# Prefix-flow step on one core: second layer's modulation vectors summed on DVE in the first MLP, norm transposes placed later

## Chip, core and metric

The kernel runs on one core of a Trainium2 chip. The metric is the device time of one execution in microseconds; the time of a kernel is the median of its runs.

## What is computed

One inference step of a flow-matching network of two layers. 1152 tokens (128 of context, 1024 latent) have 1024 channels each. A layer is a token mixer (windowed attention, gated linear attention, a gated recurrence) and an MLP with 4096 hidden channels, each behind a normalization that shift, scale and gate vectors modulate:

```python
def ada_mod(cond, w_mod, b_mod):
    mod = jax.nn.silu(cond) @ w_mod + b_mod
    mod = mod.reshape(-1, 1, 6 * D_MODEL)
    return jnp.split(mod, 6, axis=-1)

def layer(x, cond, l, P, ctx):
    sh1, sc1, g1, sh2, sc2, g2 = ada_mod(cond, P['w_mod'][l], P['b_mod'][l])
    h = rmsnorm(x, P['norm1'][l]) * (1.0 + sc1) + sh1
    mix, new_ctx = token_mixer(h, l, P, ctx)
    x = x + g1 * mix
    h = rmsnorm(x, P['norm2'][l]) * (1.0 + sc2) + sh2
    u = jax.nn.relu(h @ P['w_mlp1'][l])
    x = x + g2 * ((u * u) @ P['w_mlp2'][l])
    return x, new_ctx
```

There are two conditioning vectors, one for the context tokens and one for the latent ones. So the modulation of a layer is a product of two vectors with a 1024x6144 fp32 matrix: little arithmetic, 25 MB of weights.

## The kernel before

**Data.** x lies in SBUF as eight tiles of 128 channels by 1152 tokens. Tokens go in three blocks (tb 0 to 2) of 384. Every large product splits its fp32 operands into a high and a low part and takes three matmuls, high by high, low by high and high by low: lines L161 to L163 (`dense`), where the names hh, hl are the two parts of a normalized activation, uh, ul those of the hidden one and wh, wl those of a weight. The output projection has its own three, L1225 to L1227.

**Order.** PE's order is written by hand: it is the order in which the program emits matmuls. Small work that has to run beside the large products is written as generators that stand in `self.chain`; `tick` takes one step of the first one, and `dense` calls it every 12 matmuls. A bare `yield` is therefore "twelve matmuls later". The other engines' orders (DVE, ACT, POOL, and SP, which starts the loads) are made by a scheduler from modelled times, so an operation that is ready early can be listed far ahead of where the program emits it.

**Modulation vectors.** They are computed in three rounds of 2048 columns: round 0 gives the shift and gain of the first norm, round 1 the first gate and the second shift, round 2 the second gain and gate. `mod_round` (L246) loads, for each of eight 128-row pieces of the weight, two tiles of 128x1024 (`wm`, two buffers) and then issues four matmuls L261, one per 512 columns. In these the conditioning (`cs`, 128x32, of which two columns are filled) is the stationary operand, the weight streams, and each of the four writes 32 rows of one PSUM bank from its own 32 columns of the array:

```python
for g in range(4):
    nc.tensor.matmul(p[32 * g:32 * g + 32, :], self.cs[:, kt, :], ws[g // 2][:, 512 * (g % 2):512 * (g % 2) + 512],
                     start=kt == 0, stop=kt == KD - 1, tile_position=(0, 32 * g))
```

`mod_fin` (L265) copies the bank to SBUF (`mrow`; ACT L268, DVE L269), transposes it by four matmuls (L273) and adds the bias on DVE. For the second layer, round 0 runs in the first layer's MLP (`side_work`, one piece every eight steps), round 1 in the second layer's mixer (from the projection named gk1 to the one named k), round 2 in the second layer's attention (`side` in `layer`).

**Norms.** For one token block, `squares` (L297) squares the eight tiles on ACT and adds them on POOL and DVE (last addition L311). `norm_rs` lets two steps pass, and `rstd` (L314) then transposes the sum by three matmuls (L318) into the one PSUM bank `pe`, reduces it on DVE (L320, L321) and takes the power on POOL (L323). `spread` (L333) copies the result to 128 columns (DVE L336), lets one step pass, and transposes back (three matmuls L341; ACT copies to SBUF, L343). `norm` (L346) then makes hh and hl of each channel tile, half of them with DVE, ACT, DVE (L355 to L357), half with POOL, ACT, DVE (L359 to L363). These steps run at three borders: from attention and output projection to the MLP in both layers (`post_out`; the output projection's results are added to x by DVE, L1232), and from the first MLP to the second layer's mixer (`last_tb`).

**MLP.** `up_unit` is 24 matmuls and four operations on ACT, POOL and DVE (L1266 to L1269). `down_chunk` is 12 matmuls for each of eight output tiles and three blocks, added to x by DVE (L1290). Weights come by `load_w`: load L123 on SP, high part on ACT (L124), low part on DVE or POOL (L125), two buffers of each.

Of the kernel before, what the change touches and what calls it, by code (L numbers as in the profile page):

```python
# [15 lines left out]
KD = 8  # L16
# [33 lines left out]
class Net:  # L50
# [190 lines left out]
    def mod_round(self, l, r, psum, pool=None, slow=1):  # L241
# [20 lines left out]
                                 start=kt == 0, stop=kt == KD - 1, tile_position=(0, 32 * g))  # L262
        yield from self.mod_fin(l, r, p)

    def mod_fin(self, l, r, p):  # L265
        nc = self.nc
        m = self.wp.tile([128, 1024], F32, tag="wm", name="mrow")[:, :512]
        nc.scalar.copy(m[:, :256], p[:, :256])  # L268
        nc.vector.tensor_copy(m[:, 256:], p[:, 256:])  # L269
        yield  # L270
        p2 = self.pe()
        for j in range(4):
            nc.tensor.transpose(p2[:, 128 * j:128 * j + 128], m[:, 128 * j:128 * j + 128], self.ident)  # L273
        mt = self.const.tile([128, 4, 4, 2], F32, name=f"mod{l}_{r}")
        bm = self.V[l]["vt"][:, V_BMOD + 16 * r:V_BMOD + 16 * r + 16].rearrange("p (g j) -> p g j", g=4)
        src = p2.rearrange("p (j g s) -> p g j s", j=4, g=4)
        for s in range(2):
            nc.vector.tensor_tensor(mt[:, :, :, s], src[:, :, :, s], bm, ALU.add)
        M = self.M.setdefault(l, {})
        m = mt.rearrange("p g j s -> p (g j) s")  # L280
        if r == 0:
            M["sh1"] = m[:, 0:8]
            M["G1"] = self.gains(l, "G1", m[:, 8:16], V_N1)
        elif r == 1:
            M["g1"], M["sh2"] = m[:, 0:8], m[:, 8:16]
        else:
            M["G2"] = self.gains(l, "G2", m[:, 0:8], V_N2)
            M["g2"] = m[:, 8:16]
# [34 lines left out]
        nc.gpsimd.tensor_tensor(rs, ms, self.nhalf[:, :3], ALU.pow)  # L323
        return rs

    def norm_rs(self, x, tb, ret, alloc=None, eng0=None):
        acc = self.squares(x, tb, alloc, eng0)
        for _ in range(2):
            yield
        ret[tb] = self.rstd(acc)  # L330
        yield

    def spread(self, rs, tile):  # L333
        nc = self.nc
        bc = tile()
        nc.vector.tensor_copy(bc.rearrange("p (j c) -> p j c", j=3), rs.unsqueeze(2).to_broadcast([128, 3, 128]))  # L336
        for _ in range(1):
            yield
        pb = self.pe()
        for j in range(3):  # L340
# [5 lines left out]
    def norm(self, x, tb, ret, G, sh, hh, hl, after=None):  # L346
        nc = self.nc
        tile = self.tn
        pbs = yield from self.spread(ret[tb], tile)
        for kt, path in enumerate("ABABABAB" if tb == 0 else "ABABABAA"):  # L350
            t = tile()
            h, lo = hh(kt, tb), hl(kt, tb)
# [93 lines left out]
    def mixer(self, l):  # L446
# [519 lines left out]
        w[2] = prep(order[2][0])  # L966
        for i in range(2, len(order)):
            nm, ev, post = order[i]
            if nm == "gk1":
                self.side = self.mod_round(l, 1, self.pe, slow=4)  # L970
            elif nm == "k":
                for _ in self.side:
                    pass
                self.side = None
# [415 lines left out]

    def layer(self, l, depth):
        self.mixer(l)
        side = self.mod_round(l, 2, self.pe, slow=3)
        seq = [(0, 1), (1, 1), (2, 1), (0, 0), (1, 0), (2, 0)]
        done, state = set(), {"gen": None, "left": 0, "cur": None}
        nc = self.nc
# [42 lines left out]
        def post_out(norm2):  # L1439
# [6 lines left out]
            while out_step():  # L1446
# [2 lines left out]
                    norm2(0)  # L1449
                    added = 1  # L1450
                if added == 1 and (1, 0) not in seq and state["cur"] == (2, 0):
                    self.chain.insert(0, self.norm_rs(self.xa, 1, self.rs2, eng0=nc.vector))
                    norm2(1)
                    added = 2
                if k % 2 == 0:
                    self.tick()
            self.chain.insert(0, self.norm_rs(self.xa, 2, self.rs2, eng0=nc.vector))
            norm2(2)
            self.close(self.kg)
            self.close(self.mg)  # L1460
# [1 line left out]
        def side_work():  # L1462
            yield from self.vecs(l + 1)
            self.M[l + 1] = {}
            for r in range(1):
                yield from self.mod_round(l + 1, r, self.pe, slow=8)

        def last_tb(tb):
            if l + 1 < depth:
                if tb == 0:  # L1470
                    self.norm1(l + 1)
                    self.N1 = []
                    self.rs1 = {}
                self.add(self.norm_rs(self.xa, tb, self.rs1))
                self.N1.append(self.add(self.norm1_tb(l + 1, tb, self.rs1)))
            else:
                if tb == 0:
# [70 lines left out]
```

## Time and profile before

| | |
|---|---|
| runs | 2906.33, 2906.37, 2909.56 us |
| median | 2906.37 us |
| profiled execution | 2915.1 us |
| its span in the trace | 2913.3 us |
| mean granted clock of TensorE in it | 0.976 of full speed |
| busy in the span: PE, DVE, ACT, POOL | 94%, 50%, 38%, 27% |

The trace is of one execution. PE is TensorE's matmuls, DVE VectorE, ACT ScalarE, POOL GpSimd, and SP issues the loads. Matmul records overlap, since each includes the time in which the last columns run through the array: a 128x384 matmul has a record of 0.34 us, but the next starts 0.17 to 0.18 us after it, so the distance of starts is the price of one. L318 and the like are lines of the kernel; the name in front of `<-` is the tile that an instruction writes, those behind are the tiles it reads.

### The profile page before, as it was taken

Reading aid. Unit: us, or ns where it says so; the run is one execution under the profiler, and the core shown is the slowest. Engines: PE = TensorE matmul, PEld = TensorE weight load, DVE = VectorE, ACT = ScalarE, POOL = GpSimd, SP = SyncE. Lnnn points to the kernel's source line nnn. Section 1 sums busy time; section 2 is a strip of 40 time slices with the busy share of each in tenths; the row PEclk is TensorE's granted clock in tenths of the full one; section 3 lists DMA queues with packets and bytes.
Section 4 is the critical chain, followed back from the end, with each engine's and each line's share of the span. In section 5 each row is a group of like instructions: output and inputs, shape, how many; then the busy total and the mean of one; then the engine's idle time right before and its main releaser. Section 6 shows DMA issues by size and latency. Waiting matters only on the chain. (4 is left out here: it accounts for less than half of the span.)

```text
span 2913.3 us, 41546 instructions
## 1 busy us (share of the span) xinstructions
PE 2750.3 (94%) x16067; PEld 2626.7 (90%) x16067; DVE 1457.1 (50%) x2577; ACT 1119.5 (38%) x2046; POOL 796.9 (27%) x848
## 2 busy tenths in 40 slices
PE   5898889999999999999988989899899999999998
PEld 4887887889999999999977879878899999999998
DVE  7645677795332333233475547868832333233235
ACT  4645447764112112211356436477622112211223
POOL 4233446642001001100223244576311001100112
PEclk7999999999999999999999999999999999999999
DMA  7545348321221111111343643662211111111113
GB/s 262 136 124 158 97 150 259 122 80 58 94 84 40 44 44 44 39 42 44 111 114 91 174 126 102 209 206 79 67 43 44 44 44 37 44 44 44 43 38 130
DMA packets 279301, 273.64 MB, mean 94 GB/s; under 512 B 30032, under 2 KB 259008, under 8 KB 279104
## 3 DMA queue, kind: packets, MB, share of 16 engines
q1 hardware_dynamic: 278888, 270.92, 30.5%
q8 instruction: 127, 2.08, 0.3%
q14 instruction: 70, 0.57, 0.1%
q10 hardware_dynamic: 216, 0.06, 0.0%
HBM read 227.02 MB, written 43.91 MB: 93 GB/s over the span
## 5 line engine op out<-in xcount | busy, mean ns | idle before, releaser
L161 PE MATMUL pg<-hh,wh 128*128 128x384 f32 x1856 | 634.6, 342 | 1.8 <-ACT hh L356 1.8
L162 PE MATMUL pg<-hl,wh 128*128 128x384 f32 x1856 | 630.3, 340 | 3.1 <-DVE hl L363 1.6
L163 PE MATMUL pg<-hh,wl 128*128 128x384 f32 x1856 | 629.5, 339 | 0.0
L124 ACT CAST wh<-wr 128x1024 fp32r<-128x1024 f32 x228 | 239.0, 1048 | 914.3 <-PE pg L162 878.7
L1268 POOL TENSOR_TENSOR te<-te 128x384 f32<-128x384 f32 x192 | 166.1, 865 | 1331.3 <-ACT uh L1267 1331.0
L163 PE MATMUL pg<-uh,wl 128*128 128x384 f32 x1536 | 514.1, 335 | 1.7 <-DVE wl L125 1.7
L161 PE MATMUL pg<-uh,wh 128*128 128x384 f32 x1536 | 515.0, 335 | 0.6 <-ACT wh L124 0.6
L162 PE MATMUL pg<-ul,wh 128*128 128x384 f32 x1536 | 513.8, 335 | 0.0
L1290 DVE SCALAR_TENSOR_TENSOR x<-pg,mod,x 128x384 f32<-128x384 f32 (+2 forms) x512 | 254.2, 515 | 395.7 <-PE pg L163 395.6
L161 PEld LDWEIGHTS pg<-hh,wh 128*128 128x128 f32 x1856 | 350.6, 189 | 8.6 <-issue 5.0
L162 PEld LDWEIGHTS pg<-hl,wh 128*128 128x128 f32 x1856 | 350.8, 189 | 6.1 <-DVE hl L363 3.1
L125 DVE TENSOR_TENSOR wl<-wr,wh 128x1024 fp32r<-128x1024 f32 x196 | 244.8, 1249 | 216.3 <-ACT wh L124 216.3
L163 PEld LDWEIGHTS pg<-hh,wl 128*128 128x128 f32 x1856 | 350.3, 189 | 0.0
L1269 DVE TENSOR_TENSOR ul<-te,uh 128x384 fp32r<-128x384 f32 x192 | 107.1, 558 | 452.0 <-POOL te L1268 452.0
L161 PEld LDWEIGHTS pg<-uh,wh 128*128 128x128 f32 x1536 | 288.5, 188 | 4.3 <-issue 1.7
L163 PEld LDWEIGHTS pg<-uh,wl 128*128 128x128 f32 x1536 | 288.5, 188 | 2.3 <-DVE wl L125 2.2
L162 PEld LDWEIGHTS pg<-ul,wh 128*128 128x128 f32 x1536 | 288.5, 188 | 0.0
L1266 ACT ACTIVATE te<-pg 128x384 f32<-128x384 f32 x192 | 93.8, 489 | 358.5 <-PE pg L163 358.5
L161 PE MATMUL pd<-hh,wh 128*128 128x384 f32 x544 | 198.8, 366 | 7.8 <-DVE te L558 3.6
L162 PE MATMUL pd<-hl,wh 128*128 128x384 f32 x544 | 192.2, 353 | 3.4 <-DVE hl L397 3.4
L163 PE MATMUL pd<-hh,wl 128*128 128x384 f32 x544 | 191.4, 352 | 0.0
L1225 PE MATMUL pd<-mh,wh 128*128 128x384 f32 x384 | 137.2, 357 | 13.3 <-DVE x L1232 13.3
(293 smaller groups left out, 4216.4 us busy)
## 6 DMA issues: line engine op xcount, KB each, us to landing
wr<-in_w_mlp_dram SPq DMA_DIRECT2D x144, 512.0 KB, 4.0
wm<-in_w_mod_dram SPq DMA_DIRECT2D x96, 512.0 KB, 4.9
wr<-in_w_out_dram SPq DMA_DIRECT2D x48, 512.0 KB, 4.6
wr<-in_w_in_dram SPq DMA_DIRECT2D x36, 512.0 KB, 5.3
xd<-x SPq DMA_DIRECT2D x48, 192.0 KB, 3.8
x<-xd SPq DMA_DIRECT2D x48, 192.0 KB, 4.3
raw<-mixd SPq DMA_DIRECT2D x40, 192.0 KB, 3.0
B<-gkd SPq DMA_DIRECT2D x16, 288.0 KB, 4.7
```

Of the source, the lines that this page charges most:

```text
L124: nc.scalar.copy(hi[:, :m], raw[:, :m])
L125: lo_eng.tensor_tensor(lo[:, :m], raw[:, :m], f32(hi[:, :m]), ALU.subtract)
L161: mm(out, wh[i], xs[i][0], start=i == 0, stop=False)
L162: mm(out, wh[i], xs[i][1], start=False, stop=False)
L163: mm(out, wl[i], xs[i][0], start=False, stop=i == n - 1)
L1225: nc.tensor.matmul(p[:, :TB], wh[:, k, sl], xs[k][0], start=k == 0, stop=False)
L1266: nc.scalar.activation(r, p[:, :TB], AF.Relu)
L1268: nc.gpsimd.tensor_tensor(r, r, r, ALU.mult)
L1269: nc.vector.tensor_tensor(blk(ul, tb), r, f32(blk(uh, tb)), ALU.subtract)
L1290: nc.vector.scalar_tensor_tensor(xa, p[:, a:b], self.M[l]["g2"][:, dt, s:s + 1], xa, ALU.mult, ALU.add)
```

## The change

**The vectors.** A new `mod_vec` takes the place of `mod_round` for the second layer. It loads the weight in slabs of 128x512 (two buffers `ws` in one tile), 32 per round. For each slab DVE multiplies by one column of the conditioning and adds to a sum `macc` (128x2x512, one half for each of the two conditioning vectors): L286 for the first of eight slabs, L288 for the others, one operation for each step of the chain. After eight slabs, two fp32 matmuls L293 add the 128 partitions of each half: their stationary operand `msel` (128x2x32) holds ones in one column. Both write the same 32 rows of PSUM and use the same 32 columns of the array. There are four such pairs in a round, 17 steps apart. All three rounds now run in the first layer's MLP, one behind the other; the second layer's mixer and attention have none.

**The norms.** `norm_rs` and `spread` take the number of steps that they let pass. Token block 0's spread waits two steps in place of one. Behind the attention, block 1's sums wait three steps; block 2's squares are issued at once and its rstd goes to the end of the chain with one step of waiting, where before the whole of it was put at the chain's front. For the second layer's first norm, block 2's rstd waits four steps.

```diff
--- before.py
+++ after.py
@@ -262,6 +262,39 @@
                                  start=kt == 0, stop=kt == KD - 1, tile_position=(0, 32 * g))
         yield from self.mod_fin(l, r, p)
 
+    def mod_vec(self, l, r, mo, slow):
+        nc = self.nc
+        p = None
+        acc = self.wp.tile([128, 2, 512], F32, tag="wm", name="macc")
+        ws = self.wp.tile([128, 2, 512], F32, tag="wm", name="wm")
+
+        def load(i):
+            g, kt = divmod(i, KD)
+            c0 = r * 2048 + g * 512
+            nc.sync.dma_start(ws[:, i % 2], self.I["w_mod"][l, kt * 128:(kt + 1) * 128, c0:c0 + 512])
+
+        load(0)
+        for i in range(4 * KD):
+            g, kt = divmod(i, KD)
+            if i + 1 < 4 * KD:
+                load(i + 1)
+            for s in range(2):
+                for _ in range(slow):
+                    yield
+                c = self.cs[:, kt, s:s + 1]
+                if kt == 0:
+                    nc.vector.tensor_scalar(acc[:, s], ws[:, i % 2], c, None, ALU.mult)
+                else:
+                    nc.vector.scalar_tensor_tensor(acc[:, s], ws[:, i % 2], c, acc[:, s], ALU.mult, ALU.add)
+            if kt == KD - 1:
+                yield
+                p = p or self.pe()
+                for s in range(2):
+                    nc.tensor.matmul(p[32 * g:32 * g + 32, :], mo[:, s], acc[:, s], start=s == 0, stop=s == 1, tile_position=(0, 32 * g))
+        for _ in range(2):
+            yield
+        yield from self.mod_fin(l, r, p)
+
     def mod_fin(self, l, r, p):
         nc = self.nc
         m = self.wp.tile([128, 1024], F32, tag="wm", name="mrow")[:, :512]
@@ -323,18 +356,18 @@
         nc.gpsimd.tensor_tensor(rs, ms, self.nhalf[:, :3], ALU.pow)
         return rs
 
-    def norm_rs(self, x, tb, ret, alloc=None, eng0=None):
+    def norm_rs(self, x, tb, ret, alloc=None, eng0=None, slack=2):
         acc = self.squares(x, tb, alloc, eng0)
-        for _ in range(2):
+        for _ in range(slack):
             yield
         ret[tb] = self.rstd(acc)
         yield
 
-    def spread(self, rs, tile):
+    def spread(self, rs, tile, slack=1):
         nc = self.nc
         bc = tile()
         nc.vector.tensor_copy(bc.rearrange("p (j c) -> p j c", j=3), rs.unsqueeze(2).to_broadcast([128, 3, 128]))
-        for _ in range(1):
+        for _ in range(slack):
             yield
         pb = self.pe()
         for j in range(3):
@@ -346,7 +379,7 @@
     def norm(self, x, tb, ret, G, sh, hh, hl, after=None):
         nc = self.nc
         tile = self.tn
-        pbs = yield from self.spread(ret[tb], tile)
+        pbs = yield from self.spread(ret[tb], tile, 1 if tb else 2)
         for kt, path in enumerate("ABABABAB" if tb == 0 else "ABABABAA"):
             t = tile()
             h, lo = hh(kt, tb), hl(kt, tb)
@@ -966,9 +999,9 @@
         w[2] = prep(order[2][0])
         for i in range(2, len(order)):
             nm, ev, post = order[i]
-            if nm == "gk1":
+            if nm == "gk1" and not l:
                 self.side = self.mod_round(l, 1, self.pe, slow=4)
-            elif nm == "k":
+            elif nm == "k" and not l:
                 for _ in self.side:
                     pass
                 self.side = None
@@ -1390,7 +1423,7 @@
 
     def layer(self, l, depth):
         self.mixer(l)
-        side = self.mod_round(l, 2, self.pe, slow=3)
+        side = iter(()) if l else self.mod_round(l, 2, self.pe, slow=3)
         seq = [(0, 1), (1, 1), (2, 1), (0, 0), (1, 0), (2, 0)]
         done, state = set(), {"gen": None, "left": 0, "cur": None}
         nc = self.nc
@@ -1449,12 +1482,14 @@
                     norm2(0)
                     added = 1
                 if added == 1 and (1, 0) not in seq and state["cur"] == (2, 0):
-                    self.chain.insert(0, self.norm_rs(self.xa, 1, self.rs2, eng0=nc.vector))
+                    self.chain.insert(0, self.norm_rs(self.xa, 1, self.rs2, eng0=nc.vector, slack=3))
                     norm2(1)
                     added = 2
                 if k % 2 == 0:
                     self.tick()
-            self.chain.insert(0, self.norm_rs(self.xa, 2, self.rs2, eng0=nc.vector))
+            rs2 = self.norm_rs(self.xa, 2, self.rs2, self.te, nc.vector, slack=1)
+            next(rs2)
+            self.add(rs2)
             norm2(2)
             self.close(self.kg)
             self.close(self.mg)
@@ -1462,8 +1497,14 @@
         def side_work():
             yield from self.vecs(l + 1)
             self.M[l + 1] = {}
-            for r in range(1):
-                yield from self.mod_round(l + 1, r, self.pe, slow=8)
+            mg, mo = self.open("mo", bufs=1)
+            msel = mo.tile([128, 2, 32], F32, name="msel")
+            nc.vector.memset(msel, 0.0)
+            for s in range(2):
+                nc.vector.memset(msel[:, s, s:s + 1], 1.0)
+            for r in range(3):
+                yield from self.mod_vec(l + 1, r, msel, 1)
+            self.close(mg)
 
         def last_tb(tb):
             if l + 1 < depth:
@@ -1471,7 +1512,7 @@
                     self.norm1(l + 1)
                     self.N1 = []
                     self.rs1 = {}
-                self.add(self.norm_rs(self.xa, tb, self.rs1))
+                self.add(self.norm_rs(self.xa, tb, self.rs1, slack=2 if tb < 2 else 4))
                 self.N1.append(self.add(self.norm1_tb(l + 1, tb, self.rs1)))
             else:
                 if tb == 0:
```

In the changed kernel's numbering L318 is L351, L341 is L374, L336 is L369, L508 is L541, L1232 is L1265 and L1114 is L1147.

On PE, in the first layer's MLP, at its first `down_chunk`, before (p, cs, wm as above; `pg` is the product's PSUM bank):

```order
L161 MATMUL pg<-uh,wh 128x384
L162 MATMUL pg<-ul,wh 128x384
L163 MATMUL pg<-uh,wl 128x384
L261 MATMUL pe<-wm,cs 32x512 x4
L161 MATMUL pg<-uh,wh 128x384
```

And in the same `down_chunk` of the change:

```order
L161 MATMUL pg<-uh,wh 128x384
L162 MATMUL pg<-ul,wh 128x384
L163 MATMUL pg<-uh,wl 128x384
L293 MATMUL pe<-macc,msel 32x512 x2
L161 MATMUL pg<-uh,wh 128x384
```

Before, a group of four matmuls stands between two steps eight times in this MLP. Now a pair stands there twelve times, 17 steps from one to the next, and the 16 groups further down, in the second layer, are gone.

On DVE, at the end of the first layer's attention (L1114 splits the probabilities, L1088 is the softmax, L1139 scales the output), before:

```order
L1114 TENSOR_TENSOR pl<-pg,ph 128x512
L1099 RECIPROCAL dn<-dn 128x2
L1088 ISA P_4002,m<-pg,amask,nsink 128x512
L1088 ISA m 128x1
L1139 TENSOR_TENSOR o<-pg,ob 64x256 x2
```

And there in the change:

```order
L1147 TENSOR_TENSOR pl<-pg,ph 128x512
L1132 RECIPROCAL dn<-dn 128x2
L286 TENSOR_SCALAR macc<-wm,cs 128x512 x2
L288 SCALAR_TENSOR_TENSOR macc<-wm,cs,macc 128x512
L1172 TENSOR_TENSOR o<-pg,ob 64x256 x2
L1121 ISA P_4002,m<-pg,amask,nsink 128x512
```

The scheduler has put round 0's first three operations ahead of the MLP; the other 13 of the first pair follow among the operations of the attention's end and the output projection. The operations of the next pairs stand among the MLP's additions to x, since the one sum is free only after the pair before.

On PE, at the border from the first MLP to the second layer's mixer, block 2, before (L508 transposes a projection's result; 24 matmuls stand between the two pieces):

```order
L163 MATMUL pg<-hh_12723,wl 128x384
L318 MATMUL pe<-ident,tn 128x128 x3
L161 MATMUL pg<-hh_12716,wh 128x384
```

```order
L163 MATMUL pg<-hh_12723,wl 128x384
L341 MATMUL pe<-ident,tn 128x128 x3
L508 MATMUL pe<-ident,te 128x128 x3
L161 MATMUL pg<-hh_12716,wh 128x384
```

And in the change:

```order
L163 MATMUL pg<-hh_13012,wl 128x384
L351 MATMUL pe<-ident,tn 128x128 x3
L541 MATMUL pe<-ident,te 128x128 x3
L374 MATMUL pe<-ident,tn 128x128 x3
L161 MATMUL pg<-hh_13005,wh 128x384
```

The first transposes moved 24 matmuls down and the second ones stayed, so that no product stands between them any more.

## Rows read from the trace of the kernel before

**Rows 1.** The page: busy us, share of the span, instructions, by engine.
```profile
PE 2750.3 (94%) x16067; PEld 2626.7 (90%) x16067; DVE 1457.1 (50%) x2577; ACT 1119.5 (38%) x2046; POOL 796.9 (27%) x848
```

**Rows 2.** Windows: us, busy of PE, PEld, DVE, ACT, POOL, PEclk, DMA, GB/s.
```profile
580.00:600.00 20.00, 19.89 (x117) 18.29 (x116) 15.83 (x43) 16.13 (x36) 14.06 (x15) 1.00 0.17 54
600.00:620.00 20.00, 17.85 (x106) 16.12 (x106) 18.38 (x39) 12.19 (x29) 13.66 (x14) 1.00 0.17 53
620.00:640.00 20.00, 16.85 (x95) 16.04 (x93) 19.80 (x32) 13.49 (x27) 5.19 (x4) 1.00 0.32 106
720.00:860.00 140.00, 140.00 (x814) 132.35 (x813) 46.22 (x80) 24.65 (x38) 11.22 (x13) 1.00 0.29 91
1485.00:1500.00 15.00, 12.02 (x63) 11.69 (x62) 9.03 (x16) 6.45 (x15) 4.10 (x5) 0.89 0.09 28
1644.00:1672.00 28.00, 24.99 (x148) 22.01 (x150) 19.98 (x18) 19.25 (x43) 10.89 (x10) 0.94 0.60 179
1915.00:1945.00 30.00, 30.00 (x176) 25.21 (x176) 21.89 (x53) 20.66 (x45) 19.29 (x23) 1.00 0.52 166
1945.00:1975.00 30.00, 29.75 (x175) 23.57 (x174) 21.81 (x54) 23.04 (x50) 23.32 (x27) 1.00 0.53 170
```

**Rows 3.** PE's waits: what for, us in all, how often, longest.
```profile
PE pe L318 <- DVE tn L311: 13.4, 6, 3.0
```

**Rows 4.** Timeline of PE: start us, record us, instruction, records; first layer's MLP.
```profile
785.82 0.34 PE L162 MATMUL pg<-hl,wh 128*128 128x384 f32 x1
785.99 0.34 PE L163 MATMUL pg<-hh,wl 128*128 128x384 f32 x1
786.26 1.07 PE L261 MATMUL pe<-wm,cs 128*32 128x512 f32 x8
787.26 0.44 PE L161 MATMUL pg<-hh,wh 128*128 128x384 f32 x1
```

**Rows 5.** Groups by line and shape, PE: busy us, mean ns, idle before.
```profile
L261 PE MATMUL pe<-wm,cs 128*32 128x512 f32 x320 | 44.2, 616 | 0.0
```

**Rows 6.** The chain that ended last: start, us, step, records; final norm's transposes.
```profile
2860.79 3.57 PE pg L1335 x32
```

**Rows 7.** Groups by line and shape, DVE: busy us, mean ns, idle before, releaser.
```profile
L1290 DVE SCALAR_TENSOR_TENSOR x<-pg,mod,x 128x384 f32<-128x384 f32 x256 | 158.0, 617 | 309.4 <-PE pg L163 309.4
L1290 DVE SCALAR_TENSOR_TENSOR x<-pg,mod,x 128x256 f32<-128x256 f32 x128 | 60.8, 475 | 0.0
L1290 DVE SCALAR_TENSOR_TENSOR x<-pg,mod,x 128x128 f32<-128x128 f32 x128 | 44.8, 350 | 86.3 <-PE pg L163 86.2
L355 DVE SCALAR_TENSOR_TENSOR tn<-x,G,tn 128x384 f32<-128x384 f32 x35 | 30.0, 889 | 4.4 <-ACT tn L343 4.4
L320 DVE TENSOR_REDUCE ms<-pe 128x3 f32<-128x384 f32 x15 | 8.3, 554 | 10.2 <-PE pe L318 10.0
L336 DVE COPY tn<-rs 128x384 f32<-128x384 f32 x10 | 5.5, 552 | 6.5 <-POOL rs L323 6.5
```

**Rows 8.** The page's DMA issues: count, KB each, median us to landing.
```profile
wm<-in_w_mod_dram SPq DMA_DIRECT2D x96, 512.0 KB, 4.9
```

**Rows 9.** Timeline of PE, attention to MLP, first layer: the wait at L318.
```profile
657.49 0.34 PE L163 MATMUL pg<-hh,wl 128*128 128x384 f32 x1
660.83 0.52 PE L318 MATMUL pe<-ident,tn 128*128 128x128 f32 x3 [3.01 <-DVE tn L311]
```

**Rows 10.** Timeline of PE, the same border, first matmuls of block 2.
```profile
674.91 0.45 PE L162 MATMUL pg<-hl,wh 128*128 128x384 f32 x1 [0.66 <-DVE hl L363]
```

**Rows 11.** Timeline of PE, first MLP to second layer's mixer, block 2.
```profile
1494.15 0.52 PE L318 MATMUL pe<-ident,tn 128*128 128x128 f32 x3 [2.98 <-DVE tn L311]
1496.00 0.52 PE L162 MATMUL pg<-hl,wh 128*128 128x384 f32 x1
1500.26 0.49 PE L341 MATMUL pe<-ident,tn 128*128 128x128 f32 x3
```

**Rows 12.** Timeline of SP in the first MLP: start, us, issue.
```profile
738.08 12.86 SPq L123 DMA_DIRECT2D wr<-in_w_mlp_dram  x2
```

## Prediction

> **What bounds the kernel now.** I read the busy shares first: PE is busy for 2750.3 of 2913.3 us, DVE for half of that [rows 1]. So a microsecond of PE work in a stretch where PE never waits is a microsecond of the kernel, and DVE work there is free until DVE is full too. The windows say which stretches these are [rows 2]: in layer 0's MLP (720 to 860) PE is busy 140.00 of 140.00 us and DVE 46.22; in layer 1's attention (1915 to 1975) PE is busy 59.75 of 60. The border from attention to MLP is the opposite: from 600 to 640 DVE is busy 18.38 and 19.80 of each 20 us, PE only 17.85 and 16.85. There DVE sets the pace, and what is given to it costs time. Third, the list of PE's waits: the transposes of the norm's sums (L318) wait 13.4 us in six places for DVE's last addition [rows 3]; those are what the second half of the change aims at.
>
> **PE work removed.** A vector step of before is one group of four matmuls L261, each on 32 columns of the array. Around one, matmul starts go from 785.99 to 787.26 [rows 4]: 1.27 us where the ordinary step is 0.17 (785.82 to 785.99), so a group costs 1.10 us. 24 groups go, 26.4 us. Eight stood in layer 0's MLP, where PE is full: -8.8. Eight stood in layer 1's attention, full as well: -8.8 (bounds -8.8 and 0; its rows show no slack, so I take the end). Eight stood in layer 1's mixer; of these three lie between 1644 and 1672, where PE is busy 24.99 of 28 us [rows 2] and waits for chains of other engines that swallow the gain; five count, -5.5 (bounds -8.8 and 0). The sum is -23.1.
>
> **PE work added.** Twelve pairs of fp32 matmuls L293, 32x512, both on the same 32 columns. An fp32 matmul is two records, two passes, in this trace (x8 for four matmuls [rows 4]). The four column positions of before ran beside each other: eight records in 1.07 us, with a mean of 616 ns each [rows 5]. A pair has four passes on one position. The nearest price for passes in a row is the output's, 32 passes of 128 columns (16 matmuls) in 3.57 us, 0.1115 each [rows 6], so 0.446 for 512 columns, and 1.78 for four. The group of before must be 2 x 0.446 = 0.89 plus 0.21 for its edges; a pair then costs 1.99 us. Twelve are +23.9, all in layer 0's MLP, where PE has no slack (if the two overlapped like two positions, 1.10 each, it would be +13.2; with an edge each, 26.4). I take 23.9, since nothing in the trace overlaps on one position. The Trainium skill, TensorEngine Tiling (Array Packing), Key Properties, says that different tiles work in parallel; the trace agrees [rows 4, 5], and by that rule the change gives up its concurrency: 24 groups of eight passes become twelve of four for nearly the same PE time. The mrow transposes (L273) only move. So the vectors' PE account is -23.1 + 23.9 = **+0.8**: MLP 0 gets some 15 us longer (23.9 - 8.8), layer 1's mixer and attention 14.3 shorter.
>
> **DVE work added.** 192 operations of 128x512. L1290, of the same form, takes 350, 475 and 617 ns for 128, 256 and 384 columns [rows 7]: about 0.75 us for 512, 144 us in all. In the MLP one such operation goes beside 12 matmuls, 12 x 0.175 = 2.1 us: DVE's 46.22 of 140 [rows 2] becomes about 69%. Hidden, 0 there. The loads: a pair needs eight slabs in 17 steps, 35.9 us. A load lands 4.9 us after issue at twice the size [rows 8] and two buffers take turns, so at worst two slabs per 4.9 + 1.5 us: eight in 25.6 us, 10.3 in reserve. The new wait is the pair's, for the sum's last operation; behind it stand the MLP's own matmuls on PE, and the next quarter's first operation on DVE, as there is one sum. SP loses 48 loads of 512 KB from layer 1's mixer and attention, where L261 waited 0.0 us for them [rows 5], and takes 96 of half the size in the MLP: 0, beside weight loads that PE does not wait for there [rows 2]. The three mrow steps each get a step of 2.1 us before PE reads them: 0. But the first 16 operations, of round 0's first quarter, have no transfer from PE to wait for and the order lists them among operations that ran from 560 to 620 before: six of them, 4.5 us, in 580 to 600, where DVE has 4.2 us free, and four, 3.0 us, behind 600, where it has 1.6 and then 0.2 of 20 [rows 2]. Bounds: 0 (all fall in gaps) and 12 us (none does). I take **+4**: the last four have no place, and one or two of the six miss theirs.
>
> **The borders.** PE meets the transposes 12 or 24 matmuls later (2.1 or 4.2 us). One stall ran from 657.8 to 660.8, 3.01 us [rows 9]; with the step moved by 12 matmuls 2.1 of it is filled with work. But the stall is only worth what is not waited for afterwards. At the attention border PE comes to token block 2's first matmuls of the MLP at 674.91 and waits for hl, written by DVE [rows 10], 0.66 us and then in short steps. DVE was the later one already: a PE that arrives up to 3 us earlier waits there instead, and block 2's own rstd transposes are issued 12 matmuls later, so its hl cannot come sooner. I take -1.5 at each of the two attention borders (bounds 0 and -4.5, a third of the 13.4). At the border of the layers, PE reached the transposes at 1491.2, waited 2.98, and then ran part of the next matmuls at half clock: 0.52 us records against 0.34 [rows 11], granted clock 0.89 over 1485 to 1500 [rows 2], that is a stretch at 1.2 GHz in one otherwise at 2.4, after an engine that had stood still. Now rstd, then a projection's transposes, then the spread stand in a row behind 24 more matmuls: 1491.2 + 4.2 = 1495.4. The spread needs DVE's reduction and copy in between, at least 0.55 + 0.55 us [rows 7], POOL's power not counted, with nothing on PE to cover them: at the soonest 1496.8 against 1500.26 before, -3.5. With POOL's part unknown I take a little under the middle, -1.5 (bounds 0 and -3.5). Together **-4.5**.
>
> **The sum.** 0.8 + 4 - 4.5 = +0.3 us. It is made against the profiled execution, 2915.1 us (its span is 2913.3); the median of the runs shown is 2906.37, 8.7 lower, and I carry the difference over: 2906.7, about 2907. A measurement of this kernel tells 0.2%, 5.8 us, from no change; this is no change.
>
> **Rivals.** *The borders give all of it.* If DVE keeps up, the 13.4 us of L318 go, against +0.8 and, with DVE in time, nothing for the early operations: 2906.4 + 0.8 - 13.4 = 2894 at the best, 2898 if two thirds come. For it: the waits are real and lie on PE. Against: DVE's 92 and 99% just there, and the wait at 674.91 already standing.
>
> *The pairs are cheap.* If two matmuls on one position cost 1.10 together, the account gains 10.7: 2896. For it: the first pass's weights can be loaded beside the other's columns. Against: the passes of the output stand in a row with nothing saved [rows 6].
>
> *Slower: the early operations on DVE.* The place is layer 0's attention border. Each of the 16 operations delays hl by its length once DVE has no gaps, that is from 600 on [rows 2], and the borders give nothing because DVE is last at each: 2906.4 + 0.8 + 12 = 2919. It decides from the point where more than eight of them, 6 us, slip behind 600, which two buffers and a landing of 4.9 us [rows 8] make possible. The Trainium skill, SBUF — State Buffer, Who interferes with whom, says that a DVE instruction with two inputs in SBUF blocks and is blocked by GpSimd reading SBUF. Here L355, with two inputs in SBUF, takes 889 ns where L1290, with one in PSUM, takes 617 [rows 7]; a sum in SBUF at that ratio is 1.08 us per operation and 17 us for sixteen, so the trace bears it out as far as it goes: 2924 by that rule.
>
> *Slower: the slabs come late.* SP takes its loads in order, and one weight load stood 12.86 us at a full buffer [rows 12]. Slabs queued behind it start that much later; the reserve is 10.3 us, so a pair that meets one such stop waits about 2.6 us, twelve pairs 31 us: 2938, half of them 2922. Against: before, the same queue carried twice as large loads and L261 waited for 0.0 us.
>
> *The change doesn't do what it says* at the borders, a stall that only moves from the transposes to hl: that is inside the forecast, which gives it two thirds.
>
> **How the numbers follow.** Forecast, no change: 0.42 (its own range 2901 to 2912). Borders: 0.21. Cheap pairs: 0.11. Early DVE work: 0.15. Late slabs: 0.11. Faster is 0.21 + 0.11 = 0.32, same 0.42, slower 0.26. The range goes from 2893, just below the borders' best, to 2921, above the early operations' price and with about half of late slabs left out.
>
> **What would show it.** L293 pairs about 2.1 us apart from start to start of their neighbours, with no wait for macc; layer 0's MLP some 15 us longer; layer 1's mixer and attention some 14 shorter; L351 waiting under 5 us in all where L318 waited 13.4, and the waits for hl at block 2 (0.66 before) up to 2 or 3 us; DVE full from 560 to 640. The forecast is wrong if MLP 0 is longer by under 8 or over 20 us, if hl is waited for no longer than before, or if layer 0's attention border is over 8 us longer.

## The result, and the profile after

The changed kernel takes 2928.86 us (median; 2926.55 to 2932.83), the kernel before, on the same chip, 2907.97 us (2906.33 to 2911.37). The ratio is 1.0072, with a 95% interval of 1.0054 to 1.0089: 21 us slower, 16 to 26. The forecast was no change, 2907 us, and the result lies above its range.

The page says at once that DVE does more (1585.9 us busy against 1457.1 [rows 1]) and that PE's work is nearly what it was. The list of PE's waits, columns as in [rows 3], says where the stalls went; before, and then in the change:

```profile
PE pd L1225 <- DVE x L1232: 13.3, 5, 4.2
PE pg L1119 <- DVE pl L1114: 5.7, 12, 1.1
PE pg L162 <- DVE hl L363: 1.6, 4, 0.7
PE pg L162 <- DVE hl L357: 1.5, 3, 1.1
```

```profile
PE pd L1258 <- DVE x L1265: 17.6, 8, 4.2
PE pg L1152 <- DVE pl L1147: 6.7, 13, 1.8
PE pg L162 <- DVE hl L396: 6.4, 8, 1.2
PE pg L162 <- DVE hl L390: 3.6, 5, 1.0
PE pe L351 <- DVE te L344: 3.6, 2, 1.8
PE pe L374 <- DVE tn L369: 3.3, 2, 1.7
```

The stall that the second half of the change was made for, 13.4 us at L318 [rows 3], has come down to 0.8 us for `tn` plus the 3.6 us for `te` shown here. In its place PE waits longer for DVE in others: 10.0 us for hl in the first matmuls behind the three borders, where it had waited 3.1; 17.6 for x in the output projection (L1258), where it had been 13.3; and 3.3 at the second transposes, which before had no wait for their copy. The wait for `pl` in the attention grew by 1.0 only.

How much each stretch of the program lost is read by comparing when the same instruction starts in both traces. Two of these, ACT's seventh `relu` of each MLP, just behind the border from attention, in the kernel before and then in the change:

```profile
687.11 0.49 ACT L1266 ACTIVATE te<-pg 128x384 f32<-128x384 f32 x1 [2.40 <-PE pg L163]
...
2112.57 0.49 ACT L1266 ACTIVATE te<-pg 128x384 f32<-128x384 f32 x1 [2.39 <-PE pg L163]
```

```profile
688.39 0.49 ACT L1299 ACTIVATE te<-pg 128x384 f32<-128x384 f32 x1 [2.40 <-PE pg L163]
...
2125.69 0.49 ACT L1299 ACTIVATE te<-pg 128x384 f32<-128x384 f32 x1 [2.40 <-PE pg L163]
```

At the first the change is 1.28 us late, at the second 13.12. Five more such instructions (ACT's at 546.27, 1423.53, 1540.37, 2005.10 and 2838.67 us of the trace before) cut the program into stages; what each stage got longer or shorter, in us, worked out as the difference of two such delays:

| stage (us of the trace before) | forecast | the change | norms alone | vectors alone | vectors, held back |
|---|---|---|---|---|---|
| end of attention 0, border to MLP (546 to 687) | +2.5 | +6.6 | +3.9 | +6.6 | +1.6 |
| MLP 0 (687 to 1424) | +15.1 | +15.7 | 0.0 | +15.8 | +15.7 |
| border to layer 1 (1424 to 1540) | -1.5 | +3.5 | +2.9 | -0.7 | -1.6 |
| mixer and attention 1 (1540 to 2005) | -14.3 | -12.6 | +1.1 | -11.6 | -12.7 |
| border to MLP 1 (2005 to 2113) | -1.5 | +5.2 | +4.5 | 0.0 | -0.6 |
| MLP 1 (2113 to 2839) | 0 | +0.1 | 0.0 | +0.1 | +0.1 |
| sum | +0.3 | +18.5 | +12.4 | +10.2 | +2.6 |

Up to 546 us, where the programs do the same, the profiled execution of the change is 5.3 us ahead; that execution of before, 2915.1 us against a median of 2908, was the longer one there, so the sum from 546 on, 18.5, is the one to hold against the medians' 21. In mixer and attention 1 the runs below that leave this stage's work as it was read -3.8 to +1.1 us: a difference of that size there tells nothing.

The MLP stage is the forecast's. A pair in the changed kernel, on PE:

```profile
728.10 0.34 PE L163 MATMUL pg<-uh,wl 128*128 128x384 f32 x1
728.37 1.90 PE L293 MATMUL pe<-macc,msel 128*32 128x512 f32 x4
730.20 0.44 PE L161 MATMUL pg<-uh,wh 128*128 128x384 f32 x1
```

From 728.10 to 730.20 are 2.10 us, less an ordinary step of 0.17: 1.93 us, where a group of before cost 1.10 [rows 4]. All twelve read 2.10. (This counts up to the next start. The step behind a pair or a group is some 0.1 us longer too, here 730.20 to 730.48, so in full they cost about 2.04 and 1.20.) DVE does 81.64 us of work in 720 to 860 where it did 46.22 [rows 2], and PE waits for nothing in that MLP:

```profile
720.00:860.00 140.00, 140.00 (x775) 133.06 (x774) 81.64 (x137) 24.66 (x38) 11.79 (x13) 1.00 0.31 90
```

So the question for the experiments is why the three borders, which were to give 4.5 us and to pay 4 for the early DVE work at the first, cost 15.

### The profile page after: what moved, and what is told of

Read it like the earlier page. It is cut to its first block, busy times and chain, and to the rows that moved or that the text cites. A ratio compares the mean times of both kernels' runs of the same rounds, so it can differ in the third digit from the quotient of the medians.

```text
span 2926.5 us, 41619 instructions
## 1 busy us (share of the span) xinstructions
PE 2755.2 (94%) x15923; PEld 2627.7 (90%) x15923; DVE 1585.9 (54%) x2772; ACT 1117.2 (38%) x2044; POOL 809.9 (28%) x848
## 5 line engine op out<-in xcount | busy, mean ns | idle before, releaser
L1301 POOL TENSOR_TENSOR te<-te 128x384 f32<-128x384 f32 x192 | 172.0, 896 | 1342.6 <-ACT uh L1300 1329.4
L1323 DVE SCALAR_TENSOR_TENSOR x<-pg,mod,x 128x384 f32<-128x384 f32 (+2 forms) x512 | 253.9, 515 | 341.3 <-PE pg L163 340.3
L1258 PE MATMUL pd<-mh,wh 128*128 128x384 f32 x384 | 137.0, 357 | 17.6 <-DVE x L1265 17.6
```

The source lines that it names most:

```text
L1258: nc.tensor.matmul(p[:, :TB], wh[:, k, sl], xs[k][0], start=k == 0, stop=False)
L1301: nc.gpsimd.tensor_tensor(r, r, r, ALU.mult)
L1323: nc.vector.scalar_tensor_tensor(xa, p[:, a:b], self.M[l]["g2"][:, dt, s:s + 1], xa, ALU.mult, ALU.add)
```

## Experiments

**The two halves apart.** Norms alone: the vectors' code as before. Vectors alone: the norms' steps as before,

```diff
-        pbs = yield from self.spread(ret[tb], tile, 1 if tb else 2)
+        pbs = yield from self.spread(ret[tb], tile)
...
-                    self.chain.insert(0, self.norm_rs(self.xa, 1, self.rs2, eng0=nc.vector, slack=3))
+                    self.chain.insert(0, self.norm_rs(self.xa, 1, self.rs2, eng0=nc.vector))
...
-            rs2 = self.norm_rs(self.xa, 2, self.rs2, self.te, nc.vector, slack=1)
-            next(rs2)
-            self.add(rs2)
+            self.chain.insert(0, self.norm_rs(self.xa, 2, self.rs2, eng0=nc.vector))
...
-                self.add(self.norm_rs(self.xa, tb, self.rs1, slack=2 if tb < 2 else 4))
+                self.add(self.norm_rs(self.xa, tb, self.rs1))
```

> The norms' new places alone, the vectors as before. Theory (late transposes): DVE is the engine that is short at the borders, and its next work waits for PE's transposes, so a transpose issued later leaves DVE idle; the three borders grew by about 2, 3.5 and 5 us in the trace of the change, so +9 to +12 us over the kernel before, some 2918 us. Rival (the vectors are all of it): the norms cost nothing or gain a little, -3 to +2 us.

Measured: 2920.50 us against 2908.68, ratio 1.0046 (1.0033 to 1.0059), 13 us slower. The rival falls.

> The vectors on DVE alone, the norms as before. Theory (late transposes): the pairs cost 16 us in the first MLP, the early DVE operations 4 us in the first attention, and the second layer gives back 12, so +6 to +10 us, some 2916 us. Rival (the vectors are all of it): +18 to +21 us, some 2928 us.

Measured: 2920.72 us, ratio 1.0049 (1.0036 to 1.0062), 14 us slower; more than the 6 to 10 that was expected. Both halves cost, and neither makes the 21 us alone. By the stages the norms lose at all three borders and nowhere else, and the vectors at the end of the first attention (6.6) and in MLP 0. The rival that the vectors are all of it falls. The two sums together exceed the change's: at the first border the costs overlap (3.9 and 6.6 apart, 6.6 together).

**The sums held back.** Vectors alone, with the conditioning copied from a place that is ready only in the MLP:

```diff
+            cs = mo.tile([128, 2 * KD], F32, name="csv")
+            nc.vector.scalar_tensor_tensor(cs.rearrange("p (k s) -> p k s", k=KD), f32(uh0[:, :2 * KD]).rearrange("p (k s) -> p k s", k=KD), 0.0,
+                                           self.cs[:, :, 0:2], ALU.mult, ALU.add)
```

> As the run with the vectors alone, but the sums read a copy of the conditioning that is made from the first MLP's second hidden tile (times zero), so that no sum can run ahead of the MLP. Theory (early operations cost): 4 to 5 us faster than the vectors alone, +2 to +5 us over the kernel before. Rival (the gaps of DVE hold them): within 1.5 us of the vectors alone.

Measured: 2914.67 us, ratio 1.0024 (1.0015 to 1.0033), 6 us faster than the vectors alone on the same chip. The early operations cost that much: 6 us by the medians, 5 by the stages. (The stages of its profile add up to 2.6 where the medians are 6.0 apart; the profiled execution was itself 2.6 us under its median.) What one of them does is seen in the changed kernel, on DVE, then POOL, then PE:

```profile
561.47 2.15 DVE L288 SCALAR_TENSOR_TENSOR macc<-wm,cs,macc 128x512 f32<-128x512 f32 x1
563.54 0.68 DVE L1147 TENSOR_TENSOR pl<-pg,ph 128x512 fp32r<-128x512 f32 x1
```

```profile
560.71 2.36 POOL L125 TENSOR_TENSOR wl<-wr,wh 128x1024 fp32r<-128x1024 f32 x1 [1.94 <-ACT wh L124]
```

```profile
564.27 0.80 PE L1152 MATMUL pg<-pl,vs 128*128 128x512 f32 x1 [1.76 <-DVE pl L1147]
```

A sum of 128x512 that takes 773 ns on average in the MLP takes 2.15 us here, and ends half a microsecond behind a subtraction on POOL that had begun before it (560.71 + 2.36 = 563.07). The softmax's L1147 stands behind it on DVE, and PE waits 1.76 us for that.

The other sums of this trace show that this is no accident. Of the 168 sums L288, 136 met no operation of POOL, and each took 0.73 to 0.75 us. Seventeen began while an operation on POOL was running; sixteen of them ended 0.54 to 0.56 us after that operation, however long it was (the other kept its 0.75). Fifteen had begun before POOL's operation did, and kept their 0.73 to 0.75 us. The additions to x (L1323), which read one of their inputs from PSUM, are not stretched: 32 began under an operation of POOL and took 0.62 us at most, as without it. The next sum under a subtraction, on DVE and then POOL:

```profile
615.62 2.39 DVE L288 SCALAR_TENSOR_TENSOR macc<-wm,cs,macc 128x512 f32<-128x512 f32 x1
```

```profile
615.08 2.40 POOL L125 TENSOR_TENSOR wl<-wr,wh 128x1024 fp32r<-128x1024 f32 x1
```

The Trainium skill, SBUF — State Buffer, Who interferes with whom, says that a DVE instruction with two inputs in SBUF and a GpSimd instruction that reads SBUF exclude each other, and that the one issued first holds the port until it is done; these rows agree. No run took POOL's work away, so how much of the 6 us this accounts for is not shown.

Where the time goes can be read at the first norm's transposes back of blocks 0 and 1, before and then with the vectors alone:

```profile
617.21 0.49 PE L341 MATMUL pe<-ident,tn 128*128 128x128 f32 x3
646.83 0.49 PE L341 MATMUL pe<-ident,tn 128*128 128x128 f32 x3
```

```profile
615.09 0.50 PE L374 MATMUL pe<-ident,tn 128*128 128x128 f32 x3
647.86 0.49 PE L374 MATMUL pe<-ident,tn 128*128 128x128 f32 x3
```

At 546 us that execution was 4.8 us ahead of the one before, at the first of these transposes 2.1, at the second 1.0 behind. So 2.7 us were lost up to 617, nearly all of them just behind the sum shown above, and 3.15 between 617 and 647, where the run with the sums held back loses 0.1. The last three early sums stand at 614.85, 617.16 and 619.10 in that run and take 4.8 us together beside POOL's work, and DVE is full, in 560 to 580 nearly so and in 620 to 640 wholly:

```profile
560.00:580.00 20.00, 16.91 (x93) 14.34 (x92) 19.31 (x43) 14.79 (x32) 12.14 (x13) 1.00 0.26 79
620.00:640.00 20.00, 14.77 (x83) 13.87 (x82) 20.00 (x36) 13.53 (x27) 4.59 (x3) 0.98 0.37 113
```

So the price of an early operation has two parts: how full DVE is, and who stands behind the operation in DVE's list when POOL stretches it. In the changed kernel PE's granted clock was 0.83 over 560 to 580 as well; with the vectors alone, with the same sum of 2.16 us and the same wait of 1.8, it was 1.00, so the lower clock did not follow that wait every time.

**Which of the norms' steps.** Block 0's spread alone one step later, and block 2's rstd alone at the chain's end:

> Of the whole change only block 0's spread comes one step (12 matmuls) later, at all three borders; vectors and the other norm steps as before. Theory (a late transpose idles DVE): block 0's spread is what DVE's whole norm of block 0 waits for while DVE is the short engine, so each border loses 3 to 4 us, +8 to +12 us, most of what the norms cost together. Rival (block 2 decides, as the last thing that PE needs): 0 to +3 us.

Measured: 2923.96 us against 2909.76, ratio 1.0047 (1.0033 to 1.0061), 14 us slower; by stages +6.7, +4.5 and +3.7 at the three borders. The rival falls. (Part of the 6.7 is PE's clock, granted 0.86 and 0.91 over 620 to 640 and 640 to 660, where it was 1.00 before and with the norms together, which lost 3.9 there.)

> Only block 2 of the second norm is changed (squares at once, rstd at the chain's end); all else as before. Theory (a late transpose idles DVE, block 0's above all): this one comes when DVE has less left to do, +2 to +4 us for the two attention borders. Rival (block 2 decides): +8 to +10 us, nearly all that the norms cost together.

Measured: 2915.92 us, ratio 1.0021 (1.0012 to 1.0030), 6 us slower; +3.5 at each attention border, where at the second the waits of PE rise from 7.8 to 11.2 us in all. That is more than the theory's 2 to 4 and less than the rival's 8 to 10. Block 0's spread alone costs what the norms cost together. The two, 14 and 6, exceed the norms' 13, so either the other two moves give some 6 us back or the costs overlap. Two runs further down have those other two moves alone and are 1.5 and 1.4 us faster by them, within the noise, so that overlap is the likelier; it is not shown.

Why one step costs so much is seen at the border to MLP 1. In the kernel before, PE and then DVE:

```profile
2041.61 0.49 PE L341 MATMUL pe<-ident,tn 128*128 128x128 f32 x3
2043.92 0.44 PE L1225 MATMUL pd<-mh,wh 128*128 128x384 f32 x1 [1.82 <-DVE x L1232]
```

```profile
2040.44 0.55 DVE L336 COPY tn<-rs 128x384 f32<-128x384 f32 x1 [0.98 <-POOL rs L323]
2040.91 2.42 DVE L1202 TENSOR_TENSOR ml<-oraw,mh 128x128 fp32r<-128x128 f32 x1
2043.26 1.13 DVE L1232 SCALAR_TENSOR_TENSOR x<-pd,mod,x 128x384 f32<-128x384 f32 x2
2044.31 1.66 DVE L355 SCALAR_TENSOR_TENSOR tn<-x,G,tn 128x128 f32<-128x128 f32 x3
```

And with block 0's spread one step later:

```profile
2049.74 0.45 PE L1258 MATMUL pd<-mh,wh 128*128 128x384 f32 x1 [2.17 <-DVE x L1265]
2051.95 0.49 PE L374 MATMUL pe<-ident,tn 128*128 128x128 f32 x3
2059.58 0.66 PE L1258 MATMUL pd<-mh,wh 128*128 128x384 f32 x1 [2.96 <-DVE x L1265]
```

```profile
2046.27 0.55 DVE L369 COPY tn<-rs 128x384 f32<-128x384 f32 x1 [0.98 <-POOL rs L356]
2046.74 2.42 DVE L1235 TENSOR_TENSOR ml<-oraw,mh 128x128 fp32r<-128x128 f32 x1
2049.07 1.13 DVE L1265 SCALAR_TENSOR_TENSOR x<-pd,mod,x 128x384 f32<-128x384 f32 x2
2052.16 0.62 DVE L1265 SCALAR_TENSOR_TENSOR x<-pd,mod,x 128x384 f32<-128x384 f32 x1 [1.95 <-PE pd L1260]
2053.61 4.24 DVE L388 SCALAR_TENSOR_TENSOR tn<-x,G,tn 128x128 f32<-128x128 f32 x3 [0.83 <-ACT tn L376]
```

Before, the transposes followed DVE's copy by 1.17 us (2041.61 less 2040.44) and slipped in just ahead of a matmul that waits for DVE. One step later they stand behind that matmul and its wait of 2.17 us, and follow the copy by 5.68 us. DVE, which is the short engine here, stands idle for 1.95 and 0.83 us until they come, then does the norm in one block, three operations in 4.24 us where they had taken 1.66, and x, which stands behind it, makes PE wait 2.96 us at 2059.58, a wait the kernel before does not have. PE's stall at the first transposes did not shrink: 5.5 us at the second border, 4.7 before.

Part of the 4.24 us is POOL's: the three operations begin under a subtraction, as the sum above did, and the first of them takes 2.08. The kernel before has one there too, but it falls on two operations behind x, and PE waits for neither. On POOL with the later spread, then on POOL and DVE before:

```profile
2053.15 2.39 POOL L125 TENSOR_TENSOR wl<-wr,wh 128x1024 fp32r<-128x1024 f32 x1 [4.14 <-ACT wh L124]
```

```profile
2048.17 2.42 POOL L125 TENSOR_TENSOR wl<-wr,wh 128x1024 fp32r<-128x1024 f32 x1
2047.85 3.02 DVE L355 SCALAR_TENSOR_TENSOR tn<-x,G,tn 128x128 f32<-128x128 f32 x2
```

How the price of the late step divides between DVE's idle time and POOL's subtraction, no run separates.

**One step earlier.** To see whether the old place was merely less late:

```diff
-        pbs = yield from self.spread(ret[tb], tile)
+        pbs = yield from self.spread(ret[tb], tile, 1 if tb else 0)
```

> The kernel before with block 0's spread one step (12 matmuls) earlier in place of later. Theory (what counts is that the transpose is issued when DVE's copy is there): PE then waits some 1.5 us for the copy at each border and DVE starts the norm about 0.6 us earlier, so 0 to +4 us. Rival (the earlier the better, as the step later cost 4 us a border): -8 to -12 us.

Measured: 2907.29 us against 2908.47, ratio 0.9997 (0.9988 to 1.0006): nothing. The rival falls. PE waits for the copy as the theory had it, and its wait at the first transposes falls from 4.7 to 1.9 us; the two together give no time. At the second border:

```profile
PE pe L318 <- DVE tn L311: 1.9, 2, 1.3
PE pe L341 <- DVE tn L336: 1.5, 1, 1.5
```

Issued earlier than the copy is there, the transposes wait for it; one step later than before, they starve DVE.

**The place or the engine.** The kernel before with all rounds in MLP 0, on PE as before:

```diff
-            for r in range(1):
+            for r in range(3):
                 yield from self.mod_round(l + 1, r, self.pe, slow=8)
```

> The kernel before with all three rounds of the second layer's vectors in the first MLP, on PE as before (groups of four matmuls), none in the second layer. It tells the place from the engine. Theory: 16 groups of 1.10 us more in the MLP, +17.6, and 12 to 13 us less in the second layer, +4 to +6 us. Rival (the second layer's loads cost more than its groups, and the place alone pays): 0 or faster.

Measured: 2918.94 us, ratio 1.0036 (1.0023 to 1.0048), 10 us slower, twice what was expected. The rival falls. MLP 0 got 20.2 us longer: 16 groups of 1.20, with the longer step behind each, and some 1 us for the mrow transposes of two rounds. Layer 1 gave back 10.6. A matmul moved into this MLP costs its whole length, and where it came from it had not cost that (12.6 us on average in the kernels that took 16 groups out, for 17.6 us of groups). DVE's sums, 7 us over before when held back, are not clearly cheaper than the same move on PE, 10: their intervals overlap. With a vector step of a microsecond or more on PE, it is the move itself that loses.

**The pair's price.** The two matmuls of a pair on different column positions, quarters 2 and 3 added to other rows of the same positions:

```diff
-                    nc.tensor.matmul(p[32 * g:32 * g + 32, :], mo[:, s], acc[:, s], start=s == 0, stop=s == 1, tile_position=(0, 32 * g))
+                    q = 32 * (2 * (g % 2) + s)
+                    nc.tensor.matmul(p[q:q + 32, :], mo[:, g // 2], acc[:, s], start=g < 2, stop=g > 1, tile_position=(0, q))
```

> As the run with the vectors alone, but the two matmuls of a pair stand on different column positions of the array, so that quarters 0 and 1 fill the four positions and quarters 2 and 3 add a second row into each. Theory (a pair on one position takes its passes in a row): a pair falls from 2.0 to 1.1 us, 12 pairs give 10 to 11 us back, -1 to -4 us against the kernel before. Rival (the pair's price is its fp32 passes, wherever they stand): within 2 us of the vectors alone.

Measured: 2911.50 us, ratio 1.0013 (1.0004 to 1.0022), 9 us faster than the vectors alone on the same chip. The same four records now take 1.05 us in place of 1.90:

```profile
1151.03 0.34 PE L163 MATMUL pg<-uh,wl 128*128 128x384 f32 x1
1151.30 1.05 PE L294 MATMUL pe<-macc,msel 128*32 128x512 f32 x4
1152.28 0.45 PE L161 MATMUL pg<-uh,wh 128*128 128x384 f32 x1
```

1.25 us from 1151.03 to 1152.28, less 0.17: 1.08. MLP 0 is 5.6 us longer than before in place of 15.8. The rival falls. The Trainium skill, TensorEngine Tiling (Array Packing), Key Properties, says that different tiles of the array can multiply in parallel; the two records agree.

**Together, and a version that beats both.** Two positions and the sums held back; then the same with the two norm moves left that are neither block 0's spread nor block 2's second norm:

> The vectors alone, with the pair on two column positions and the sums held back to the MLP: the two gains of the first runs, 6 and 9 us, are in different stretches and add up. From the vectors alone (+12 us) that gives -3 to -5 us against the kernel before, some 2904 us. Rival (the early operations and the pairs share a cost): +1 to +3 us.

Measured: 2903.75 us, ratio 0.9972 (0.9960 to 0.9984), 8 us faster than before (6 by the medians), where 3 to 5 was expected. The rival falls. The two gains add up, and to more than their sum: from 1.0049 they would give 0.9988, just outside the interval; mixer and attention 1, the stage that varies, was 16.0 us shorter in the profiled execution.

> As the run with both mends of the vectors, plus the two norm changes that DVE does not wait for at once: block 1's sums three steps in the second norm, block 2's rstd four steps in the second layer's first norm. Theory: these are the steps with which PE's stall shrinks and DVE is not starved, 2 to 5 us faster than without them, -5 to -10 us against the kernel before. Rival (every later transpose costs): 0 to 4 us slower than without them.

Measured: 2902.22 us, ratio 0.9967 (0.9955 to 0.9978). 1.5 us faster than without them, inside the intervals: neither theory is shown.

Then each sum in two halves of 256 columns, so that four matmuls fill the four positions:

```diff
+                for h in range(2):
+                    for s in range(2):
+                        q = 32 * (2 * h + s)
+                        nc.tensor.matmul(p[q:q + 32, :256], mo[:, 31 - g:63 - g], acc[:, s, 256 * h:256 * h + 256], start=g == 0, stop=g == 3, tile_position=(0, q))
```

> As the run with both mends of the vectors, but each sum of 512 columns is split in two halves of 256, so that four matmuls (two halves, two conditioning vectors) stand on the four column positions; a shifted selector puts quarter g into row g of each, and the transposes fall from four to two per round. Theory (positions run beside each other, passes on one in a row): a step costs 2 x 0.22 + 0.21 = 0.66 us in place of 1.2, 6 to 7 us faster than with two positions, -13 to -16 us against the kernel before. Rival (a step's price is its edges, not its columns): within 2 us of two positions.

Measured: 2898.93 us against 2908.47, ratio 0.9968 (0.9958 to 0.9978), 9 us faster than before, not the 13 to 16 that were expected. The step itself is right to the hundredth:

```profile
1138.32 0.34 PE L163 MATMUL pg<-uh,wl 128*128 128x384 f32 x1
1138.59 0.64 PE L295 MATMUL pe<-macc,msel 128*32 128x256 f32 x8
1139.16 0.45 PE L161 MATMUL pg<-uh,wh 128*128 128x384 f32 x1
```

0.84 less 0.17 is 0.67 us, and MLP 0 is as long as before (-0.1 in place of +5.6). So the rival's reason falls, though the total came out within its 2 us of two positions. The rest is in the stages that vary between kernels: with two positions mixer and attention 1 happened to be 16.0 us shorter, here 14.6, and the first border is 1.9 longer, there 0.3. Whether the total is better than with two positions is open.

> The same with block 1's sums three steps in the second norm and block 2's rstd four steps in the second layer's first norm. Theory: these two moves gave 1.5 us within the noise, so this stays within 3 us of the run without them. Rival (they help where DVE is not starved): 4 us faster or more.

Measured: 2897.58 us, ratio 0.9963 (0.9951 to 0.9976), 11 us faster than before and 31 faster than the change, the best here; the two norm moves again stay within what the runs can tell.

## Why the prediction was wrong

- **PE's price of the vectors** was right. A pair was put at 1.99 us and measures 1.93; MLP 0 was to be 15.1 longer (in the forecast's words "some 15") and is 15.7. Left out were the longer step behind each group and pair and the mrow transposes of two rounds, which come into this MLP, some 1.3 us; the pairs' price, 0.7 too high in all, makes up for half of that. Layer 1 was to give 14.3 back and gave 12.6, which is also the mean of the eight kernels with DVE sums (9.6 to 16.0); the 1.7 that are missing are within what this stage varies by.
- **DVE's work in the MLP** was hidden as forecast: DVE waited 18.6 us for slabs and 8.4 for pairs there, and none of it reached PE. The rival of the late slabs falls with that.
- **The early operations** had the right place and too small a size: +4, measured 5 to 6. The forecast's "the last four have no place" behind 600 is borne out by the 3.15 us lost between 617 and 647 with the vectors alone. What it did not price is POOL: a sum by itself takes 0.75 us, as forecast, but these last four took 0.95 to 2.39, each begun under an operation of POOL, and the one at 563 cost 2.6 us of PE's time in a stretch for which the forecast counted no loss. The rival of the early work put a sum at 1.08 us by the mean of L355; that mean mixes 0.60 us alone and up to 1.4 under POOL's operations.
- **The borders are the step that failed**: -4.5 with bounds of 0 and about -12.5, measured +13 for the norms alone. The forecast asked what a stall is worth to PE, found that little, and so took zero as the worst. It did not ask who waits for the transposes. DVE does, on the one stretch where the forecast itself had DVE as the short engine: with block 0's spread alone one step later, 14 us are lost, and at the border to MLP 1 DVE idles 1.95 and 0.83 us and PE then waits 2.96 for x. The bound on the other side should have come from there: the transposes at 2041.61 stood just ahead of a matmul that waits 1.82 us for DVE, and one step later they stand behind it. The forecast's own sign, L351 waiting under 5 us (4.4 for block sums in `tn` and `te`), came true while the borders lost 15: the stall had moved, not gone.
- That block 2's hl could not come sooner was right; that it would come later, with a price of 3.5 us at each attention border, was not drawn from it.
- At the border of the layers the forecast had rstd and spread meet with nothing between and still gave a gain of 1.5. It measured +2.9 with the norms alone, and +4.5 of block 0's spread alone. In the two runs that keep block 2's rstd four steps late and leave block 0's spread where it was, the border is as long as before (0.0), so the meeting itself neither gave nor cost. (The earliest time there, 1495.4 + 0.55 + 0.55, is 1496.5 and not 1496.8; and of the 48 loads that leave SP, 32 stood in layer 1 and 16 in MLP 0. Neither changes the forecast.)

## What to carry to other kernels

An instruction on the full engine may be the input of another engine that is just as full for that moment: before moving it later to spare a wait, look at when its result is first used and at what stands between the old place and the new one. If one of the instructions between them waits, the moved one waits with it, and the engine that it feeds stands idle and passes the delay on. And work given to an engine with idle time is only free where its order lets it be: here operations that were ready early were listed early, ahead of work that others waited for, until something held them back.

## What the runs showed that was not expected

Two fp32 matmuls on one column position take 1.93 us, on two positions 1.08, and four of half the width on four positions 0.67: the same columns in a third of the time, by how they are split and placed. And a DVE sum with both inputs in SBUF that began under an operation of POOL ended about 0.55 us after it, sixteen times of seventeen: 0.75 us became up to 2.39, and PE, which stood behind one of them, waited 1.76.
